# Hybrid attention trunk: V of two head groups in 512-column products, one value product per pair of heads, later steps, norm weights loaded elsewhere

## The chip, the core and the metric

The kernel runs on one core of a Trainium2 chip. Its engines are TensorE (PE in the profile, with PEld for its weight loads), VectorE (DVE), ScalarE (ACT), GpSimd (POOL) and SyncE (SP, which here only issues transfers). Each has its own instruction stream and works through it in order; they meet through semaphores. The metric is the device time of one execution in microseconds (us), lower is better. The kernel before takes 869.72 us, the median of three runs (869.27 to 870.09).

## The reference, cut to what matters

Two layers over 512 positions of width 1024, all float32. In each, one projection feeds three groups of heads:

```python
h = rms_norm(x, g_pre)
qa, ka, va, ga, qs, ks, vs, gs, qf, kf, vf, gf, ff = split(h @ w_in)      # 12 x 512 columns, and 8
# a) differential: 4 heads, rotary on part of q and k, two softmax maps each
w  = softmax(mask(q0 k0)) - lam * softmax(mask(q1 k1));  ya = rms_norm(w @ v) * (1 - lambda_init) * silu(ga)
# b) stick-breaking: 8 heads, strictly causal
a  = exp(log_sigmoid(z) + sum of log_sigmoid(-z) over later keys);        yb = (a @ v) * silu(gs)
# c) forgetting: 8 heads, causal softmax with a cumulative log gate as bias
p  = softmax(q k * scale + cum_q - cum_k);                                yc = (p @ v) * silu(gf)
x  = x + rms_norm(concat(ya, yb, yc) @ w_out, g_post)
```

## The kernel before, in words

A layer runs through stages named after the group whose columns are being projected: a, c, b, then the gates, then the output projection. `hT` holds the normalised input, transposed, as a high and a low part, and so does each weight; one product is three matmuls (`mm3`, L200 to L202). `proj_N` makes V 256 columns at a time for 128 positions, in eight chunks of the inner dimension; `proj_V` makes 512 columns at a time, and before the change only group b used it. `proj_T` makes q and k transposed, 128 columns by 512 positions. Every accumulation has one of three PSUM buffers `pj`.

Weights come in "halves" of 512 KB: a transfer on SP's queue into `raw` (3 buffers), a copy on ACT that rounds it to the high part (`split_to`, L184), and on POOL four subtractions for the low part (L190), into `hl` (4 buffers). A V unit for `proj_V` is four such halves, each with two chunks of the inner dimension.

While one group is projected, the attention steps of the group before run in between: 16 steps, four heads or pairs of heads by four blocks `i` of 128 queries. A step makes scores (L364), works on them on DVE and ACT, turns the weights with PE transposes into PSUM (L372), and an eviction writes them to SBUF (`pT`; group c: ACT for the first head, DVE at L377 for the second). Then `pair_av` multiplies them by v (L462, plain float32, the two heads on two halves of the array): before the change once for the blocks 0 and 1 and once for 2 and 3, with 256 columns. In stage a the rotary embedding keeps DVE busy (L328 to L332), ACT then writes the high part of q or k (L344) and DVE the low part (L349).

The order on every engine is written out by hand: `do` puts projection work in a row with a cost, `at` hangs side work at a time on that axis, and all is sorted by time. `use` says when a half is first needed, and its `lead` how much earlier its split is hung in. So a number in the code sets the order of instructions, not a time on the chip.

At the start `first_gain` loads the row of norm weights and spreads it over the partitions by matmul (L607); for the post norm `new_post` loads the weights that the evictions of the output projection need (L791).

Of the kernel before, what the change touches and what calls it, by code (L numbers as in the profile page):

```python
# [17 lines left out]
S = 512  # L18
# [42 lines left out]
def hybrid_kernel(ctx, tc, x, w_in, forget_bias, diff_lambda, diff_subln, w_out, pre_norm, post_norm, consts, out):  # L61
# [10 lines left out]
    t2_p = P("t2", T2_BUFS)  # L72
    pt0_p = P("pT0", 2)
    pt1_p = P("pT1", 2)
    cb_p = P("cb", 2)
# [32 lines left out]
    def load_rope():  # L108
        a, b = CONST_COLS["rope"]
        C["rope"] = pt1_p.tile([128, 2, S], F32, name="rope", tag="pT1")  # L110
        nc.sync.dma_start(out=C["rope"], in_=consts[:, a:b])
# [126 lines left out]

    def proj_V(k0, tt, hT, done):

        st = {}
        sl = slice(tt * 128, (tt + 1) * 128)

        def go(q):
            if q == 0:
                st["ps"] = pj_p.tile([128, S], F32, name="pj", tag="pj")
            h = hT()
            for kc in range(2 * q, 2 * q + 2):
                u = halves[k0 + q]["hl"][:, :, kc % 2]
                mm3(st["ps"], h[0][:, kc, sl], h[1][:, kc, sl], u[:, 0], u[:, 1], kc == 0, kc == KC - 1)  # L250

        for q in range(4):
            do(1296, lambda q=q: go(q))
        at(now[0], lambda: done(st["ps"]))

# [60 lines left out]

    def load_gain(g, src):
        for h, t in enumerate(g):
            nc.sync.dma_start(out=t, in_=src[h * S:(h + 1) * S].partition_broadcast(128))

# [79 lines left out]
    def step_a(t, c, h, i):  # L400
# [16 lines left out]
        def turn():  # L417
            st["t"] = t = pt0_p.tile([128, 4, 128], F32, name="wT", tag="pT0")
            transposed(st["p", 0], i, t[:, 0:i + 1], "act")
# [29 lines left out]
    def turned(c, pi, m, i):  # L449

        if i % 2 == 0:
            c["t", pi, i // 2, m] = (pt0_p if i == 0 else pt1_p).tile([128, i + 2, 256], F32, name="pT", tag=f"pT{i // 2}")
        return c["t", pi, i // 2, m][:, 0:i + 1, (i % 2) * 128:(i % 2 + 1) * 128]

    def pair_av(c, v, oT, pi, i, gated=False):
        ts = [c["t", pi, i // 2, m] for m in range(2)]
        o = ov_p.tile([128, 256], F32, name="ov", tag="ov")
        for j in range(i + 1):
            q0 = 128 if j == i else 0
            for m in range(2):  # L460
# [3 lines left out]
        d = oT[:, pi, (i - 1) * 128:(i + 1) * 128]  # L464
# [43 lines left out]
    def step_b(t, c, pi, i):  # L508
# [32 lines left out]
        for m in range(2):  # L541
# [5 lines left out]
            at(d + 5400, lambda m=m: turn(m))  # L547
        if i % 2:
            ta = max(t + 10900, c["gate"][pi])
            at(ta, lambda: pair_av(c, v(), oT(), pi, i, gated=True))  # L550
            if i == NT - 1:
                at(ta + 1200, lambda: c["cut"](pi))

# [36 lines left out]
    def first_norm(L):  # L590
# [7 lines left out]
        def first_gain():  # L598

            row = pt1_p.tile([1, 2, S], F32, name="grow", tag="pT1")  # L600
            nc.scalar.dma_start(out=row.rearrange("p h c -> p (h c)"), in_=pre_norm[0:1])
# [10 lines left out]
        t = -40000  # L612
        at(t, lambda: nc.vector.memset(mhalf, -0.5))
        at(t, lambda: load(0))
        at(t, first_gain)
        at(t, lambda: load_to(1))
        at(t, load_ident)
        at(t, lambda: L["st", 0].update(g=L["g"]))
# [13 lines left out]
    def plan_layer(l, L):  # L632
# [9 lines left out]
        for g in ("a", "c", "b"):  # L642
# [8 lines left out]
            if prev is not None:  # L651
                pst, pc, pg = prev
                at(t0, lambda pst=pst: pst.update(o=o_p.tile([128, 4, S], F32, name="o" + pg, tag="o")))
                steps(step_a if pg == "a" else step_c, pc, t0 + (3518 if pg == "a" else 3191), 50075 if pg == "a" else 46774)
            order = [(u, tt) for u in range(2) for tt in range(NT)]
            if g == "a":
                order = [(0, 0), (0, 1), (0, 2), (1, 0), (1, 1), (1, 2), (0, 3), (1, 3)]
            ks = []
            if g == "b":
                order = []  # L660
                kv = add_v_unit(l, base + 1024)
                for h in range(4):
                    use(kv + h, now[0] + 1296 * h)
                for tt in range(NT):
                    proj_V(kv, tt, hT, lambda ps, st=st, tt=tt: nc.scalar.activation(out=st["v"][:, tt], in_=ps, func=AF.Copy))
            for u in range(2 if g != "b" else 0):
                ks.append(add_in_unit(l, base + 1024 + u * UW, 6144 if g == "a" and u == 0 else None))
# [26 lines left out]
            for u in range(2):  # L694
                for part in ("q", "k"):
# [6 lines left out]
                    if g == "b" and u == 0 and part == "q":  # L702
                        for h in range(2):
                            halves[k0 + h]["lead"] = (3800, 5100)[h]
# [65 lines left out]
        for u, (g, j0) in enumerate(order):  # L770
            k = add_out_unit(l, row[g] + j0, 0, whl_p, "whl")
            use(k, now[0])
            for jj in range(2):
                for tt in range(NT) if (u, jj) == (5, 1) else (3, 0, 1, 2):
# [9 lines left out]
                    if u == 5 and jj == 1:  # L784
                        def ev(tt=tt):
                            if tt % 2 == 0:
                                L["yh"] = pt1_p.tile([128, 2, S], F32, name="y0", tag="pT1")
                            L["y0", tt] = t = L["yh"][:, tt % 2]
# [28 lines left out]
        for tt in range(NT):  # L817
# [98 lines left out]
```

## Time and profile before

| what | value |
|---|---|
| median of three runs | 869.72 us |
| profiled execution | 870.16 us, of which the span 868.1 us |
| TensorE busy, matmuls | 852.5 us (98%), 4700 instructions |
| VectorE busy | 496.4 us (57%) |
| ScalarE busy | 475.9 us (55%) |
| GpSimd busy | 447.7 us (52%) |
| mean granted TensorE clock | 0.998 |

The span goes from the first to the last instruction. A row of the timeline gives start, duration, engine, line, operation and tiles; "x8" after it says that eight like instructions are merged in the row, and brackets at its end give the engine's idle time before it and what ended it. Durations of neighbouring matmuls overlap, so what a matmul costs is read from the distance between two starts. A float32 matmul of `pair_av` shows as two instructions.

### The profile page before, as it was taken

To read this page: it belongs to the slowest core of one execution; us is meant where nothing else is said; L and a number is where in the kernel's file an instruction comes from. 1 tells how busy PE (TensorE), PEld (TensorE's weight loads), DVE (VectorE), ACT (ScalarE), POOL (GpSimd) and SP (SyncE) were. 2 spreads that over 40 slices of the span, in tenths; PEclk is the share of its full clock that TensorE was granted. 3 is DMA by queue.
4 is the path that set the end of the run, shared out by engine and by line. 5 is a ranking of instruction groups with operands and counts; after the bars stand their busy time and mean duration, and the time that the engine had idled before them with its cause. 6 is when DMAs were issued, how large, how long until landed. Compare 5 with 4: busy or idle time off the path is not lost.

```text
span 868.1 us, 13536 instructions
## 1 busy us (share of the span) xinstructions
PE 852.5 (98%) x4700; PEld 711.0 (82%) x4700; DVE 496.4 (57%) x1143; ACT 475.9 (55%) x1056; POOL 447.7 (52%) x678
## 2 busy tenths in 40 slices
PE   7999999999999999999999999999999999999997
PEld 5988998888878787788898889888888787877885
DVE  5378656544555777623653875664445477774322
ACT  4344667757775556633334356675677756664310
POOL 3366554645544548770364664556274544678301
PEclk9999999999999999999999999999999999999999
DMA  7354323432523321237253452325244422122522
GB/s 236 96 163 134 94 81 91 118 101 80 154 76 105 85 61 53 71 117 247 96 177 98 122 146 74 98 73 162 59 131 113 120 54 71 49 81 89 167 100 97
DMA packets 71157, 94.24 MB, mean 109 GB/s; under 512 B 6433, under 2 KB 52129, under 8 KB 71090
## 3 DMA queue, kind: packets, MB, share of 16 engines
q1 hardware_dynamic: 68784, 89.19, 35.2%
q10 hardware_dynamic: 2306, 4.20, 1.6%
q8 instruction: 37, 0.61, 0.3%
q14 instruction: 30, 0.25, 0.1%
HBM read 76.56 MB, written 4.23 MB: 93 GB/s over the span
## 4 chain that ended last, share of the span: by engine, by line
PE 81%; DVE 10%; ACT 3%; DMA 2%; issue 2%; POOL 1%; DVEq 0%; POOLq 0%; ACTq 0%
PE pj L200 18%; PE pj L202 18%; PE pj L201 18%; PE s L364 7%; PE pt L372 5%; PE ov L462 5%; PE acc L200 2%; PE acc L202 2%; PE acc L201 2%; PE ov L424 2%; DVE ra L332 2%; DVE sh L331 2%; DVE sh L328 1%; DVE qd L349 1%; DVE ra L330 1%
## 5 line engine op out<-in xcount | busy, mean ns | idle before, releaser
L190 POOL TENSOR_TENSOR hl<-raw,hl 128x256 fp32r<-128x256 f32 (+1 forms) x418 | 341.1, 848 | 217.4 <-ACT hl L184 193.2
L200 PE MATMUL pj<-hT,hl 128*128 128x512 f32 x576 | 236.4, 410 | 0.0
L202 PE MATMUL pj<-hT,hl 128*128 128x512 f32 x576 | 225.7, 392 | 0.0
L201 PE MATMUL pj<-hT,hl 128*128 128x512 f32 x576 | 225.2, 391 | 0.0
L184 ACT ACTIVATE hl<-raw 128x1024 fp32r<-128x1024 f32 (+1 forms) x120 | 126.3, 1058 | 35.2 <-DMA raw<-in_w_out_dram 18.7
L202 PEld LDWEIGHTS pj<-hT,hl 128*128 128x128 f32 x576 | 108.1, 188 | 24.2
L200 PEld LDWEIGHTS pj<-hT,hl 128*128 128x128 f32 x576 | 108.4, 188 | 20.0 <-issue 2.1
L201 PEld LDWEIGHTS pj<-hT,hl 128*128 128x128 f32 x576 | 108.7, 189 | 17.0
L200 PE MATMUL pj<-hl,hT 128*128 128x256 f32 (+2 forms) x320 | 101.0, 316 | 0.3 <-ACT hT L282 0.2
L202 PE MATMUL pj<-hl,hT 128*128 128x256 f32 (+2 forms) x320 | 98.4, 308 | 0.5 <-DVE hT L283 0.5
L201 PE MATMUL pj<-hl,hT 128*128 128x256 f32 (+2 forms) x320 | 98.2, 307 | 0.0
L398 ACT ACTIVATE p<-p,mn 128x128 f32<-128x128 f32 (+3 forms) x128 | 71.0, 555 | 33.0 <-DVE mn L389 31.1
L531 DVE TENSOR_TENSOR_SCAN kp<-kp,c_masks 128x128 f32<-128x128 f32 (+3 forms) x64 | 67.3, 1051 | 18.6 <-ACT kp L524 18.1
L364 PE MATMUL s<-kd,qd 128*128 128x128 f32 (+1 forms) x192 | 61.9, 327 | 2.8 <-DVE mn L389 2.8
L200 PEld LDWEIGHTS pj<-hl,hT 128*128 128x128 f32 x320 | 61.4, 192 | 3.4 <-ACT hT L282 1.0
L202 PEld LDWEIGHTS pj<-hl,hT 128*128 128x128 f32 x320 | 61.1, 191 | 3.8 <-DVE hT L283 1.2
L375 ACT ACTIVATE pT<-pt 128x128 f32<-128x128 f32 (+3 forms) x96 | 41.2, 443 | 41.8 <-PE pt L372 41.6
L201 PEld LDWEIGHTS pj<-hl,hT 128*128 128x128 f32 x320 | 61.4, 192 | 2.6 <-POOL hl L190 0.6
L364 PE MATMUL s<-kd,qs 128*128 128x128 f32 (+1 forms) x192 | 61.1, 322 | 0.0
L536 DVE TENSOR_TENSOR sg<-sg,kp 128x127 f32<-128x127 f32 (+3 forms) x64 | 46.1, 720 | 5.5
L481 POOL TENSOR_TENSOR cm<-cb,c_causal 128x128 f32<-128x128 f32 x64 | 28.2, 461 | 38.6 <-DMA cb<-cs 21.2
L193 DVE TENSOR_TENSOR hl<-raw,hl 128x1024 fp32r<-128x1024 f32 (+3 forms) x18 | 21.4, 1199 | 44.7 <-ACT hl L184 44.5
(143 smaller groups left out, 1456.9 us busy)
## 6 DMA issues: line engine op xcount, KB each, us to landing
raw<-in_w_in_dram SPq DMA_DIRECT2D x96, 512.0 KB, 3.7
qs<-qd SPq DMA_DIRECT2D x48, 256.0 KB, 4.3
raw<-in_w_out_dram SPq DMA_DIRECT2D x24, 512.0 KB, 3.5
cb<-cs ACTq DMA_DIRECT2D x16, 256.0 KB, 3.2
xl<-in_x_dram SPq DMA_DIRECT2D x4, 512.0 KB, 5.4
xt<-in_x_dram SPq DMA_DIRECT2D x8, 256.0 KB, 6.3
xs<-xt SPq DMA_DIRECT2D x8, 256.0 KB, 2.0
xt<-xs SPq DMA_DIRECT2D x8, 256.0 KB, 2.8
```

The source lines that it names most:

```text
L184: nc.scalar.activation(out=hl[:, 0], in_=raw, func=AF.Copy)
L190: nc.gpsimd.tensor_tensor(out=hl[:, 1, k, c:e], in0=raw[:, k, c:e], in1=hl[:, 0, k, c:e].bitcast(F32), op=ALU.subtract)
L200: nc.tensor.matmul(out=ps, lhsT=lh, rhs=rh, start=first, stop=False)
L201: nc.tensor.matmul(out=ps, lhsT=lh, rhs=rl, start=False, stop=False)
L202: nc.tensor.matmul(out=ps, lhsT=ll, rhs=rh, start=False, stop=last)
L364: nc.tensor.matmul(out=s[:, 0:n], lhsT=pr[q][:, m, i * 128:n], rhs=pr["k"][:, m, 0:n], start=(j == 0), stop=(j == 1))
L372: nc.tensor.transpose(out=pt[:, j * 128:(j + 1) * 128], in_=p[:, j * 128:(j + 1) * 128], identity=C["ident"])
L375: nc.scalar.activation(out=t, in_=src, func=AF.Copy)
L398: nc.scalar.activation(out=p[:, 0:n], in_=p[:, 0:n], func=AF.Exp, bias=st["mn", m], scale=-1.0, accum_out=su)
L462: nc.tensor.matmul(out=o[H[m], q0:256], lhsT=v[:, j, col:col + 64], rhs=ts[m][:, j, q0:256], start=(j == 0), stop=(j == i))
L531: nc.vector.tensor_tensor_scan(out=rv, data0=rv, data1=C["first"][:, S - n:S][:, ::-1], initial=0.0, op0=ALU.mult, op1=ALU.max)
L536: nc.vector.tensor_tensor(out=sg[:, 0:n - 1], in0=sg[:, 0:n - 1], in1=kp[:, 1:n], op=ALU.mult)
```

## The change

Group c's V is made by `proj_V` too, so 256-column products of that group become half as many of 512 columns; group a keeps `proj_N`. `proj_V` takes two blocks of positions at a time and goes over the first half of the inner dimension for both before it goes on to the second half, and the leads of the third and fourth half of the unit change (at the same places on the axis as before for group b, whose use is later now). `pair_av` runs once per pair of heads with up to 512 columns, on weights that lie in one tile per head. The differential steps start 2982 units later in stage c and are 2775 units shorter in all; the forgetting steps turn their weights 1339 units later, and their value product comes 7600 units after the start of the last step. Three pools of SBUF become one. The first norm row goes on SP's queue, ahead of x, the identity ahead of the first weights; the post-norm weights go on ACT's queue and 3000 units earlier; the next layer's norm transposes come 949 units later.

```diff
-    def proj_V(k0, tt, hT, done):
+    def proj_V(k0, tts, hT, done):
...
+        for q in (0, 2):
+            for tt in tts:
+                for j in range(2):
+                    do(1296, lambda tt=tt, q=q + j: go(tt, q))
+                if q == 2:
+                    at(now[0], lambda tt=tt: done(ps[tt], tt))
...
     def turned(c, pi, m, i):
-        if i % 2 == 0:
-            c["t", pi, i // 2, m] = (pt0_p if i == 0 else pt1_p).tile([128, i + 2, 256], F32, name="pT", tag=f"pT{i // 2}")
-        return c["t", pi, i // 2, m][:, 0:i + 1, (i % 2) * 128:(i % 2 + 1) * 128]
-
-    def pair_av(c, v, oT, pi, i, gated=False):
-        ts = [c["t", pi, i // 2, m] for m in range(2)]
-        o = ov_p.tile([128, 256], F32, name="ov", tag="ov")
-        for j in range(i + 1):
-            q0 = 128 if j == i else 0
+        if i == 0:
+            c["t", pi, m] = pt_w.tile([128, 13 * 128], F32, name="pT", tag="pT")
+        d = c["t", pi, m][:, i * 128:(i + 1) * 128]
+        return bass.AP(tensor=d.tensor, offset=d.offset, ap=[d.ap[0], [384, i + 1], [1, 128]])
+
+    def pair_av(c, v, oT, pi, gated=False):
+        ts = [c["t", pi, m] for m in range(2)]
+        o = ov_p.tile([128, S], F32, name="ov", tag="ov")
+        for j in range(NT):
             for m in range(2):
                 col = (2 * pi + m) * 64
-                nc.tensor.matmul(out=o[H[m], q0:256], lhsT=v[:, j, col:col + 64], rhs=ts[m][:, j, q0:256],
-                                 start=(j == 0), stop=(j == i))
+                nc.tensor.matmul(out=o[H[m], j * 128:S], lhsT=v[:, j, col:col + 64],
+                                 rhs=ts[m][:, j * 512:j * 384 + 512], start=(j == 0), stop=(j == NT - 1))
...
-            at(d + 4261, lambda m=m: turn(m))
-        if i % 2:
-            at(t + 9959, lambda: pair_av(c, v(), oT(), pi, i))
+            at(d + 5600, lambda m=m: turn(m))
+        if i == NT - 1:
+            at(t + 7600, lambda: pair_av(c, v(), oT(), pi))
...
-            ta = max(t + 10900, c["gate"][pi])
+            ta = max(t + 8500, c["gate"][pi])
...
-        at(t, lambda: load(0))
         at(t, first_gain)
+        at(t, lambda: load(0))
+        at(t, load_ident)
         at(t, lambda: load_to(1))
-        at(t, load_ident)
...
-                steps(step_a if pg == "a" else step_c, pc, t0 + (3518 if pg == "a" else 3191), 50075 if pg == "a" else 46774)
+                steps(step_a if pg == "a" else step_c, pc, t0 + (6500 if pg == "a" else 3191), 47300 if pg == "a" else 46774)
...
-            if g == "b":
+            if g != "a":
                 order = []
                 kv = add_v_unit(l, base + 1024)
+                by = 2
                 for h in range(4):
-                    use(kv + h, now[0] + 1296 * h)
+                    if by == 2:
+                        halves[kv + h]["lead"] = (9500, 8000, 7700, 6400)[h]
+                    use(kv + h, now[0] + 1296 * (h + (2 if by == 2 and h > 1 else 0)))
...
-            load_gain(gains["post"], post_norm[l])
-        at(now[0] - 9000, new_post)
+            load_gain(gains["post"], post_norm[l], nc.scalar)
+        at(now[0] - 12000, new_post)
...
-                for d, fn in zip((2500, 4500, 4600, 7551, 8326), pre_norm_stages(st, tt, N["hT"])):
+                for d, fn in zip((2500, 4500, 4600, 8500, 9275), pre_norm_stages(st, tt, N["hT"])):
```

What moves on ACT at the passage from stage a to stage c of the first layer: `kd` is the high part of a k projection (the third and the fourth of the last two units), `hl` with L184 or L183 a half of V's weights, `v` an eviction of V. Before:

```order
L344 ACTIVATE kd_878<-ra_861 64x512 x2
L184 ACTIVATE hl_916<-raw_763 128x1024
L344 ACTIVATE kd_936<-ra_897 64x512 x2
L681 ACTIVATE v_901<-pj_903 128x256
L184 ACTIVATE hl_961<-raw_823 128x1024
```

And now:

```order
L346 ACTIVATE kd_875<-ra_858 64x512 x2
L183 ACTIVATE hl_884<-raw_760 128x1024
L183 ACTIVATE hl_915<-raw_820 128x1024
L346 ACTIVATE kd_929<-ra_902 64x512 x2
L400 ACT_TABLE_LOAD
```

The third half of V stands where it stood, behind the last but one k; the fourth now stands next to it, ahead of the last k.

PE at the same place, one row for each half of the weights as it is first used by a block of positions (hl_817, 845, 916 and 961 are the four halves before, hl_814, 842, 884 and 915 now; `pj` with a new number is a new accumulation, `s` are the first scores of the differential steps). Before:

```order
L200 MATMUL pj_903<-hl_817,hT0_145 128x256
...
L200 MATMUL pj_903<-hl_845,hT0_145 128x256
...
L364 MATMUL s_955<-kd_696,qd_594 128x128
...
L364 MATMUL s_981<-kd_696,qd_594 128x128
...
L364 MATMUL s_1005<-kd_696,qd_594 128x256
```

And now:

```order
L199 MATMUL pj_908<-hl_814,hT0_142 128x512
...
L199 MATMUL pj_908<-hl_842,hT0_142 128x512
...
L199 MATMUL pj_932<-hl_814,hT0_142 128x512
...
L199 MATMUL pj_908<-hl_884,hT0_142 128x512
...
L199 MATMUL pj_908<-hl_915,hT0_142 128x512
...
L366 MATMUL s_959<-kd_693,qd_591 128x128
...
L199 MATMUL pj_932<-hl_884,hT0_142 128x512
```

Before, the third half was first used after all four blocks of positions had used the first two, 96 products of 256 columns on; now it is used after two blocks, 24 products of 512 columns on, and the fourth half 6 products later. The first scores now come after both.

PE around a value product of group c in stage b (`pt` the transposes of the second head's last block, `ov` the value product, `s` scores of the next pair). Before, the second of two products of a pair:

```order
L462 MATMUL ov_2587<-pT_2395,v_901 64x256
L462 MATMUL ov_2587<-pT_2405,v_901 64x256
...
L462 MATMUL ov_2587<-pT_2395,v_901 64x128
L462 MATMUL ov_2587<-pT_2405,v_901 64x128
```

And now, the only one:

```order
L374 MATMUL pt_2384<-c_masks_128,p_2281 128x128 x4
L366 MATMUL s_2395<-kd_1682,qd_1449 128x256
L366 MATMUL s_2395<-kd_1682,qs_1475 128x256
L199 MATMUL pj_2292<-hl_2060,hT0_142 128x512
...
L464 MATMUL ov_2422<-pT_2220,v_906 64x512
L464 MATMUL ov_2422<-pT_2234,v_906 64x512
L464 MATMUL ov_2422<-pT_2220,v_906 64x384
L464 MATMUL ov_2422<-pT_2234,v_906 64x384
```

Between the last transposes and the value product there now stand two score matmuls of 256 columns and six products of 512.

## Rows read from the trace of the kernel before

**Rows 1.** The page: busy time by engine, and the granted clock in 40 slices.

```profile
PE 852.5 (98%) x4700; PEld 711.0 (82%) x4700; DVE 496.4 (57%) x1143; ACT 475.9 (55%) x1056; POOL 447.7 (52%) x678
PEclk9999999999999999999999999999999999999999
```

**Rows 2.** Waits of PE, one line: for whom, us in total, times, longest.

```profile
PE s L364 <- DVE mn L389: 2.8, 2, 1.7
```

**Rows 3.** Timeline of PE: V in 256 columns, products 1 and 24; 512 columns, 11 in a row.

```profile
36.70 0.28 PE L200 MATMUL pj<-hl,hT 128*128 128x256 f32 x1
...
39.45 0.28 PE L202 MATMUL pj<-hl,hT 128*128 128x256 f32 x1
...
195.66 0.39 PE L201 MATMUL pj<-hl,hT 128*128 128x512 f32 x1
...
197.96 0.39 PE L202 MATMUL pj<-hl,hT 128*128 128x512 f32 x1
```

**Rows 4.** Timeline of PE: two value products, what stands before and behind them.

```profile
208.77 1.74 PE L462 MATMUL ov<-pT,v 128*64 128x256 f32 x16
210.44 0.66 PE L372 MATMUL pt<-c_masks,p 128*128 128x128 f32 x4
...
287.26 0.40 PE L202 MATMUL pj<-hT,hl 128*128 128x512 f32 x1
287.58 0.87 PE L462 MATMUL ov<-pT,v 128*64 128x256 f32 x8
288.38 0.50 PE L200 MATMUL pj<-hT,hl 128*128 128x512 f32 x1
288.72 0.40 PE L201 MATMUL pj<-hT,hl 128*128 128x512 f32 x1
```

**Rows 5.** Timeline, all engines: from stage a to c in layer one, then two.

```profile
83.59 0.28 PE L200 MATMUL pj<-hl,hT 128*128 128x256 f32 x1
84.42 1.28 ACT L344 ACTIVATE kd<-ra 64x512 fp32r<-64x512 f32 x2 [3.24 <-DVE ra L332]
85.72 1.06 ACT L184 ACTIVATE hl<-raw 128x1024 fp32r<-128x1024 f32 x1
86.86 3.72 POOL L190 TENSOR_TENSOR hl<-raw,hl 128x256 fp32r<-128x256 f32 x4 [1.88 <-ACT hl L184]
92.47 0.38 PE L364 MATMUL s<-kd,qd 128*128 128x256 f32 x1 [1.09 <-DVE mn L389]
92.87 2.84 POOL L190 TENSOR_TENSOR hl<-raw,hl 128x256 fp32r<-128x256 f32 x4 [2.30 <-ACT hl L184]
...
508.39 0.28 PE L200 MATMUL pj<-hl,hT 128*128 128x256 f32 x1
512.32 3.73 POOL L190 TENSOR_TENSOR hl<-raw,hl 128x256 fp32r<-128x256 f32 x4 [1.89 <-ACT hl L184]
517.93 0.38 PE L364 MATMUL s<-kd,qd 128*128 128x256 f32 x1 [1.75 <-DVE mn L389]
```

**Rows 6.** Timeline: PE behind post-norm weights, then ahead of layer two.

```profile
403.93 0.50 PE L200 MATMUL pj<-hl,yv 128*128 128x512 f32 x1 [0.25 <-DVE y L791]
...
439.40 0.63 PE L279 MATMUL pt<-c_masks,xn 128*128 128x128 f32 x4 [0.66 <-DVE xn L273]
```

**Rows 7.** Timeline of SP's queue: issues of the first x and of the identity.

```profile
0.72 0.39 SPq L594 DMA_DIRECT2D xl<-in_x_dram  x1
...
2.97 0.51 SPq L106 DMA_DIRECT2D c_masks<-in_consts_dram  x1
```

**Rows 8.** Timeline: last transposes of two forgetting pairs, and their eviction on DVE.

```profile
201.30 0.62 PE L372 MATMUL pt<-c_masks,p 128*128 128x128 f32 x4
201.96 0.69 DVE L377 COPY pT<-pt 128x512 f32<-128x512 f32 x1
...
221.12 0.62 PE L372 MATMUL pt<-c_masks,p 128*128 128x128 f32 x4
222.97 0.69 DVE L377 COPY pT<-pt 128x512 f32<-128x512 f32 x1
```

More of the change, by code (lines that the diff above doesn't have):

```diff
@@ L72, in hybrid_kernel @@
     t2_p = P("t2", T2_BUFS)
-    pt0_p = P("pT0", 2)
-    pt1_p = P("pT1", 2)
+    pt_w = P("pT", 2)
     cb_p = P("cb", 2)
@@ L109, in load_rope @@
         a, b = CONST_COLS["rope"]
-        C["rope"] = pt1_p.tile([128, 2, S], F32, name="rope", tag="pT1")
+        C["rope"] = pt_w.tile([128, 2, S], F32, name="rope", tag="pT")
         nc.sync.dma_start(out=C["rope"], in_=consts[:, a:b])
@@ L237, in proj_N, with go @@
             at(now[0] + t, fn)
-    def proj_V(k0, tt, hT, done):
-        st = {}
-        sl = slice(tt * 128, (tt + 1) * 128)
-        def go(q):
+    def proj_V(k0, tts, hT, done):
+        ps = {}
+        def go(tt, q):
             if q == 0:
-                st["ps"] = pj_p.tile([128, S], F32, name="pj", tag="pj")
+                ps[tt] = pj_p.tile([128, S], F32, name="pj", tag="pj")
             h = hT()
+            sl = slice(tt * 128, (tt + 1) * 128)
             for kc in range(2 * q, 2 * q + 2):
                 u = halves[k0 + q]["hl"][:, :, kc % 2]
[L250 to L254, printed above, removed]
+                mm3(ps[tt], h[0][:, kc, sl], h[1][:, kc, sl], u[:, 0], u[:, 1], kc == 0, kc == KC - 1)
+        for q in (0, 2):
[4 more added lines that the diff above has]
+                    at(now[0], lambda tt=tt: done(ps[tt], tt))
     def pre_norm_stages(st, tt, hT):
@@ L315, in new_gain, with load_gain @@
         return [t[:, 0], t[:, 1]]
-    def load_gain(g, src):
+    def load_gain(g, src, eng=nc.sync):
         for h, t in enumerate(g):
-            nc.sync.dma_start(out=t, in_=src[h * S:(h + 1) * S].partition_broadcast(128))
+            eng.dma_start(out=t, in_=src[h * S:(h + 1) * S].partition_broadcast(128))
     H = (slice(0, 64), slice(64, 128))
@@ L417, in turn @@
         def turn():
-            st["t"] = t = pt0_p.tile([128, 4, 128], F32, name="wT", tag="pT0")
+            st["t"] = t = pt_w.tile([128, 4, 128], F32, name="wT", tag="pT")
             transposed(st["p", 0], i, t[:, 0:i + 1], "act")
@@ L547, in step_b @@
             at(d + 5400, lambda m=m: turn(m))
-        if i % 2:
-            ta = max(t + 10900, c["gate"][pi])
-            at(ta, lambda: pair_av(c, v(), oT(), pi, i, gated=True))
-            if i == NT - 1:
-                at(ta + 1200, lambda: c["cut"](pi))
+        if i == NT - 1:
+            ta = max(t + 8500, c["gate"][pi])
+            at(ta, lambda: pair_av(c, v(), oT(), pi, gated=True))
+            at(ta + 2000, lambda: c["cut"](pi))
     def decay(ff, lc, l):
@@ L598, in first_gain @@
         def first_gain():
-            row = pt1_p.tile([1, 2, S], F32, name="grow", tag="pT1")
-            nc.scalar.dma_start(out=row.rearrange("p h c -> p (h c)"), in_=pre_norm[0:1])
+            row = pt_w.tile([1, 2, S], F32, name="grow", tag="pT")
+            nc.sync.dma_start(out=row.rearrange("p h c -> p (h c)"), in_=pre_norm[0:1])
             one = t1_p.tile([1, 128], F32, name="one", tag="on")
@@ L613, in first_norm @@
         at(t, lambda: nc.vector.memset(mhalf, -0.5))
+        at(t, first_gain)
         at(t, lambda: load(0))
-        at(t, first_gain)
+        at(t, load_ident)
         at(t, lambda: load_to(1))
-        at(t, load_ident)
         at(t, lambda: L["st", 0].update(g=L["g"]))
@@ L658, in plan_layer @@
             ks = []
-            if g == "b":
+            if g != "a":
                 order = []
                 kv = add_v_unit(l, base + 1024)
+                by = 2
                 for h in range(4):
-                    use(kv + h, now[0] + 1296 * h)
-                for tt in range(NT):
-                    proj_V(kv, tt, hT, lambda ps, st=st, tt=tt: nc.scalar.activation(out=st["v"][:, tt], in_=ps, func=AF.Copy))
-            for u in range(2 if g != "b" else 0):
+                    if by == 2:
+                        halves[kv + h]["lead"] = (9500, 8000, 7700, 6400)[h]
+                    use(kv + h, now[0] + 1296 * (h + (2 if by == 2 and h > 1 else 0)))
+                for t_ in range(0, NT, by):
+                    proj_V(kv, range(t_, t_ + by), hT,
+                           lambda ps, tt, st=st: nc.scalar.activation(out=st["v"][:, tt], in_=ps, func=AF.Copy))
+            for u in range(2 if g == "a" else 0):
                 ks.append(add_in_unit(l, base + 1024 + u * UW, 6144 if g == "a" and u == 0 else None))
@@ L701, in plan_layer @@
                             halves[k0 + h].update(lead=2500, lo="both")
-                    if g == "b" and u == 0 and part == "q":
+                    if g != "a" and u == 0 and part == "q":
                         for h in range(2):
@@ L786, in ev @@
                             if tt % 2 == 0:
-                                L["yh"] = pt1_p.tile([128, 2, S], F32, name="y0", tag="pT1")
+                                L["yh"] = pt_w.tile([128, 2, S], F32, name="y0", tag="pT")
                             L["y0", tt] = t = L["yh"][:, tt % 2]
```

2 lines of the change are left out of this document (1 added, 1 removed).

## The prediction

> **What bounds the kernel now.** I read the page first: TensorE's matmuls are busy for 852.5 of the span's 868.1 us, at full granted clock (2.4 GHz) in every slice, while VectorE, ScalarE and GpSimd stand at 52 to 57% [rows 1]. So the kernel is bound by the row of instructions on PE: whatever shortens that row, or a wait in it, comes off the time one for one, and what happens elsewhere counts only where PE comes to wait for it. Next I read PE's waits: the largest that the change touches is that of the scores L364 for DVE, 2.8 us in two waits [rows 2]. Then the timeline of PE, for what one instruction costs there (distances between starts, since durations overlap). Last the timeline of all engines at the passage from stage a to c, because there the change moves weights and work at once.
>
> **The change part by part.**
>
> *V of group c.* Per layer 192 products of 256 columns become 96 of 512. From product 1 to product 24 in 256 columns it is 39.45 - 36.70 = 2.75 us in 23 steps, 0.1196 us each; in 512 columns 2.30 us in 10 steps, 0.230 each [rows 3]. Two layers: 384 x 0.1196 = 45.9 against 192 x 0.230 = 44.2, so -1.7 us, all on PE's row.
>
> *One value product per pair.* There were 32 groups (two for each of 4 pairs, 2 head groups, 2 layers), now 16. The columns are the same in sum, 384 + 896 = 1280 per head. A group of 384 took 288.38 - 287.58 = 0.80 us, one of 896 took 210.44 - 208.77 = 1.67 [rows 4]; that is 1.70 ns per column and 0.15 us that each group pays whatever its size. Around it PE pays for going in, 287.58 - 287.26 = 0.32 where 0.23 is usual, and for coming out into a product, 288.72 - 288.38 = 0.34 where 0.23 is usual [rows 3, 4]: 0.09 and 0.11. A group saved is worth 0.24 (where transposes follow, whose own extra I put at nothing) to 0.35 us, so 3.8 to 5.6 for 16; I take -5.2, nearer the upper end, because by the order all 16 that remain are followed by products, and of the 32 old ones 18 by products or scores and 14 by transposes. No row shows a float32 product of 512 columns. If width has a price of its own, the gain could be nothing; that is the other end.
>
> *Differential steps later.* The two waits of L364 on DVE are 1.09 and 1.75 us of idle time [rows 5]; a score there starts 0.16 us later still than the idle time says, because a product of 256 lasts 0.28 but is followed after 0.12 [rows 3]. Together -3.1 us. DVE is through with the rotary work in both layers before the scores in their new place come, so this wait goes.
>
> *What is late next there.* This is the step that decides. PE begins V of group c at 83.59 us. The third half of the weights is split by ACT only at 85.72, right behind the k that waited 3.24 us for DVE, and POOL subtracts from 86.86 to 90.58 [rows 5]. Before, PE wanted that half after 96 products; now it wants it after 24 products of 512, and the fourth after 30. ACT's order keeps the third half where it was and puts the fourth next to it, ahead of the last k. POOL then goes straight on with the fourth half: another 2.84 us (the row at 92.87) or 3.72 (the row at 86.86), so it ends at 93.4 to 94.3. PE, were it not held, would need its last piece after 33 products, at 83.59 + 33 x 0.230 = 91.2. So PE is held for 2.2 to 3.1 us. In the second layer the start is 508.39 and POOL ends with the third half at 512.32 + 3.73 = 516.05 [rows 5]; the same sum gives 518.9 to 519.8 against 516.0, 2.9 to 3.8 us. Together 5.1 to 6.9; I take +5.7. If ACT or POOL came to these halves earlier than the order says, it would be nothing.
>
> *Post-norm weights and norm transposes.* PE idled 0.25 us for L791, which waited for the weights' transfer, and 0.66 us in the transposes L279 [rows 6]; a product of 512 lasts 0.39 and is followed after 0.23 [rows 3], so each costs 0.16 more: 0.4 and 0.8. The weights now come 3000 units earlier (13 products) and the transposes 949 units later (4 products, 0.9 us), so both go: -1.2 us. The two issues on ACT's queue stand in the output projection, where PE waits for no ACT work in the rows; if they did not hide there, they would cost twice the 0.5 us of such an issue [rows 7].
>
> *Start.* One more issue stands on SP's queue ahead of x. Issues of this kind took 0.39 and 0.51 us [rows 7], and x is what everything at the start waits for: +0.45. The identity ahead of the first weights delays them by 0.5 more, and if that counts too it is 0.9; if the earlier row of weights helps, nothing.
>
> *Forgetting steps.* Turning later costs nothing by itself. But the value product follows its last transposes closely now: 0.46 for these (0.62 less the 0.16 of overlap), two scores of 0.12, six products of 0.23 and 0.09 for going in, 2.2 us from the start of the transposes. The eviction on DVE ended 1.35 us after that start in one pair (201.30 to 202.65) and 2.54 in another (221.12 to 223.66) [rows 8]. So the wait is 0 or 0.34 us; for eight such groups 0 to 2.7, and I take +0.4, since the shorter lag is the usual one. Stick-breaking has by the order some five products more there in three pairs of four and is hidden. The merged pools and the two blocks at a time in V of group b change no order that PE waits on: its halves are split where they were and used later.
>
> Sum: -1.7 - 5.2 - 3.1 + 5.7 - 1.2 + 0.45 + 0.4 = -4.65. The profiled execution took 870.16 us (span 868.1 and 2.06 around it), 0.44 above the median of 869.72. Off the median the forecast is 865.1 us, or 865.5 for an execution like the profiled one.
>
> **The rivals.**
>
> *The halves come in time.* If ACT reaches the third and fourth half before the k that waits for DVE, or DVE is further along, the +5.7 falls away: -10.35, 859.4 us. For it speaks that POOL idled 1.88 us before the third half; against it that ACT works in order and stood still for DVE until 84.42 [rows 5].
>
> *Both halves at the slow pace.* A group of four subtractions took 3.72 us beside DVE's rotary work and 2.84 without it [rows 5]. While POOL does the fourth half, DVE still has the low part of the last k to do, so 3.72 may hold for it too: 6.9 instead of 5.7, 866.3 us. The Trainium skill, SBUF — State Buffer, section Who interferes with whom, says that a DVE instruction with two inputs in SBUF holds up a GpSimd instruction that reads SBUF, and the other way round, for a whole instruction; the trace agrees with it in the two durations, and by that rule it would be this case.
>
> *Slower: the value product waits for POOL.* In stage b the diagonal bias of the next scores is added on POOL, behind weight splits of 2.84 us, and DVE, in order, then makes the eviction late; the copy at 222.97 came 1.0 us later after its transposes than that at 201.96 [rows 8] for a reason of this kind. Should each of the eight forgetting groups find a whole split in front, its eviction ends 1.35 + 2.84 = 4.2 us after the transposes and PE waits 2.0: 16 in place of 0.4, 880.7 us. From 0.85 us a group on, the kernel is slower than before. Against it: the larger lag shown is 2.5, not 4.2.
>
> *The wide value product saves nothing.* Without the -5.2 it is +0.55, 870.3 us.
>
> **How the numbers follow.** The forecast gets 0.53, its own range being 862.5 to 867.5; the halves in time 0.20; the slow pace 0.15; waiting for POOL 0.07; no gain from width 0.05. The range goes from 859.4, the first rival, to 867.9, which leaves out the last two and little else. A measurement of this kernel can tell 0.2%, some 1.7 us. Faster by more than that: the first three, less a little of their upper tail, 0.87; within it 0.06; slower 0.07.
>
> **What would show it.** L200 to L202 in 256 columns 384 fewer, and 16 groups of the value product, each near 2.3 us. No wait of L364 for DVE; in its place waits of L200 and L201 for POOL's subtraction in the first blocks of V of group c, 2 to 4 us in each layer. The first transposes 0.4 to 0.5 us later. No wait at L791's release. If PE shows no wait for POOL there, the forecast is wrong and the first rival right; if a group of the value product stays above 2.5 us or starts behind a wait for the eviction, the last two are.

## The result, and the profile after

The changed kernel takes 881.32 us, the median of four runs (880.05 to 884.92), against 869.70 us (869.27 to 870.09): 1.0138 times the time before, 95% interval 1.0125 to 1.0151. It is slower; 865.1 us was forecast. The profiled execution took 880.05 us, its span is 878.1, 10.0 more than before.

First the span in stages, by the start of PE's first product in each: layer one, V of group c, the q and k products of c, V of group b, and the stretch from there to the output projection. Columns: span, then busy time and instructions of PE, weight loads, DVE, ACT and POOL, granted clock, DMA share, GB/s. Before:

```profile
83.59:115.14 31.55, 30.37 (x250) 29.79 (x248) 17.97 (x57) 20.35 (x53) 16.24 (x24) 1.00 0.31 89
115.14:177.41 62.27, 62.27 (x337) 53.17 (x336) 40.03 (x125) 42.46 (x115) 34.30 (x59) 1.00 0.39 105
177.41:207.29 29.88, 29.88 (x157) 24.72 (x156) 12.65 (x61) 19.02 (x48) 13.39 (x25) 1.00 0.21 66
207.29:370.46 163.17, 163.14 (x903) 129.52 (x903) 104.11 (x218) 104.84 (x230) 96.69 (x149) 1.00 0.32 91
```

After:

```profile
84.37:115.03 30.66, 28.44 (x141) 23.11 (x140) 17.03 (x49) 18.07 (x45) 13.60 (x19) 1.00 0.22 59
115.03:184.59 69.56, 65.21 (x348) 53.89 (x347) 40.86 (x132) 44.47 (x120) 37.47 (x66) 1.00 0.40 109
184.59:215.82 31.23, 31.23 (x165) 25.18 (x164) 13.06 (x62) 18.82 (x47) 15.89 (x28) 1.00 0.26 79
215.82:376.10 160.28, 159.82 (x834) 125.61 (x833) 100.03 (x210) 104.69 (x230) 91.27 (x143) 1.00 0.32 90
```

The loss is in the first two rows: stage c grew from 93.82 to 100.22 us, and PE's idle time in its q and k products from 0 to 4.35. The other two rows together shrank, from 193.05 to 191.51. In layer two stage c grew from 94.50 to 101.79.

PE's waits of the changed kernel (whom for, us in total, times, longest) against [rows 2]:

```profile
PE pj L200 <- POOL hl L189: 4.7, 7, 0.9
PE pt L374 <- DVE p L416: 4.4, 6, 1.0
PE pt L442 <- DVE oc L443: 2.9, 4, 0.7
...
PE pt L374 <- ACT wT L377: 1.2, 2, 0.6
...
PE s L366 <- DVE mn L391: 0.9, 2, 0.5
```

The first line is the wait for the weight halves that was forecast (one of the seven, 0.3 us, stands at the start of the kernel). The two waits of the scores for DVE, 2.8 us, are gone; the 0.9 in the last line (L366 is the old L364) are two new ones of 0.46, in the forgetting steps, shown below. The second, third and fourth line were not forecast: transposes of the differential steps, L374 for the weights and L442 for the output, that wait for DVE and ACT. But DVE is 55% busy. What it waits for there, before and after:

```profile
DVE on L427 <- PE pt L440: 17.7, 12, 4.5
```

```profile
DVE on L429 <- PE pt L442: 38.0, 16, 4.5
```

`on` is the output row of a differential step, and has three buffers. L429 writes it at 7856 units of a step, L442 reads it last at 17029. Where three steps follow each other within 9173 units, DVE's write of step n+3 stands, by the order, behind a transpose of step n that PE has further down its row. By the step lengths in the code three steps took 8450 to 10328 units before, under 9173 at 7 of 13 places in a layer; now they take 7982 to 9756, under it at 10. One such place in the timeline, ACT, DVE and PE in turn (start, duration, instruction, idle time before it); the row of ACT is the normalisation of `on`, which had waited for GpSimd, and two of the experiments are about that:

```profile
118.58 0.40 ACT L438 ACTIVATE on<-on,rsub 128x128 f32<-128x128 f32 x1 [2.98 <-POOL rsub L126]
```

```profile
121.44 0.35 DVE L429 TENSOR_SCALAR on<-ov,r 128x128 f32<-128x128 f32 x1 [3.38 <-PE pt L442]
121.71 0.15 DVE L411 RECIPROCAL r<-su 128x1 f32<-128x1 f32 x1
...
122.69 0.91 DVE L416 SCALAR_TENSOR_TENSOR p<-p,rho 128x256 f32<-128x256 f32 x1
...
124.48 0.34 DVE L443 TENSOR_SCALAR oc<-pt,sub 128x128 f32<-128x128 f32 x1
```

```profile
121.13 0.27 PE L442 MATMUL pt<-c_masks,on 128*128 128x128 f32 x1
...
123.75 0.41 PE L374 MATMUL pt<-c_masks,p 128*128 128x128 f32 x2 [0.95 <-DVE p L416]
124.87 0.33 PE L442 MATMUL pt<-c_masks,on 128*128 128x128 f32 x1 [0.72 <-DVE oc L443]
```

DVE stands still for 3.38 us until PE reaches L442 at 121.13, and then has the reciprocals, L416 and two score reductions to do in a row. PE, six products further, comes to the transposes that need them and waits twice. So PE waits for an engine that had waited for PE.

The wait that was forecast in V of group c, on PE and on POOL:

```profile
90.49 0.39 PE L199 MATMUL pj<-hl,hT 128*128 128x512 f32 x1
91.38 0.50 PE L200 MATMUL pj<-hl,hT 128*128 128x512 f32 x1 [0.50 <-POOL hl L189]
...
93.21 0.50 PE L200 MATMUL pj<-hl,hT 128*128 128x512 f32 x1 [0.87 <-POOL hl L189]
...
95.03 0.50 PE L200 MATMUL pj<-hl,hT 128*128 128x512 f32 x1 [0.85 <-POOL hl L189]
```

```profile
87.61 7.37 POOL L189 TENSOR_TENSOR hl<-raw,hl 128x256 fp32r<-128x256 f32 x8 [1.89 <-ACT hl L183]
```

By starts, against 0.23 a product, PE loses 0.66, 1.04 and 1.02 us: 2.7 a layer. The product behind each wait is followed after 0.34 in place of 0.23, which makes it 3.0. And one value product of a pair of heads, which answers to [rows 4]:

```profile
211.30 2.37 PE L464 MATMUL ov<-pT,v 128*64 128x512 f32 x16
213.60 0.50 PE L199 MATMUL pj<-hl,hT 128*128 128x512 f32 x1
```

One wait was not forecast there either, in the forgetting steps, on POOL, DVE and PE:

```profile
226.30 2.81 POOL L189 TENSOR_TENSOR hl<-raw,hl 128x256 fp32r<-128x256 f32 x4 [1.87 <-ACT hl L183]
229.07 2.12 POOL L483 TENSOR_TENSOR cm<-cb,c_causal 128x128 f32<-128x128 f32 x5
```

```profile
229.56 0.29 DVE L391 CUSTOM_DVE_ANT_0 p<-s,cm 128x128 f32<-128x128 f32 x1 [0.81 <-POOL cm L483]
```

```profile
229.92 0.39 PE L366 MATMUL s<-kd,qd 128*128 128x256 f32 x1 [0.46 <-DVE mn L391]
```

The diagonal bias `cm` stands on POOL behind a weight split, DVE waits for it, and the next scores on PE wait for DVE: once in each layer.

### The profile page after: what moved, and what is told of

It is laid out like the page before. It is cut to its first block, busy times and chain, and to the rows that moved or that the text cites. A ratio compares the mean times of both kernels' runs of the same rounds, so it can differ in the third digit from the quotient of the medians.

```text
span 878.1 us, 12845 instructions
## 1 busy us (share of the span) xinstructions
PE 852.6 (97%) x4380; PEld 694.8 (79%) x4380; DVE 487.2 (55%) x1127; ACT 474.3 (54%) x1048; POOL 443.4 (50%) x678
## 4 chain that ended last, share of the span: by engine, by line
PE 78%; POOL 10%; issue 6%; DVE 3%; ACT 2%; DMA 1%; SPq 0%; DVEq 0%; POOLq 0%; ACTq 0%
PE pj L199 18%; PE pj L201 17%; PE pj L200 17%; POOL hl L189 9%; PE s L366 6%; PE pt L374 5%; PE ov L464 4%; PE acc L199 2%; PE acc L200 2%; PE acc L201 2%; PE ov L426 2%; ACT hl L183 1%; DVE p L391 1%; DVE p L416 1%; DMA raw<-in_w_in_dram 1%
## 5 line engine op out<-in xcount | busy, mean ns | idle before, releaser
L199 PE MATMUL pj<-hT,hl 128*128 128x512 f32 x576 | 236.6, 411 | 0.0
L183 ACT ACTIVATE hl<-raw 128x1024 fp32r<-128x1024 f32 (+1 forms) x120 | 125.8, 1056 | 39.5 <-DMA raw<-in_w_out_dram 21.9
L199 PEld LDWEIGHTS pj<-hT,hl 128*128 128x128 f32 x576 | 108.6, 188 | 21.0 <-issue 2.4
L200 PE MATMUL pj<-hl,hT 128*128 128x512 f32 (+2 forms) x256 | 88.7, 346 | 4.7 <-POOL hl L189 4.7
L199 PE MATMUL pj<-hl,hT 128*128 128x512 f32 (+2 forms) x256 | 91.0, 356 | 1.0 <-ACT hT L284 1.0
L400 ACT ACTIVATE p<-p,mn 128x128 f32<-128x128 f32 (+3 forms) x128 | 71.0, 555 | 36.1 <-DVE mn L391 35.3
L201 PE MATMUL pj<-hl,hT 128*128 128x512 f32 (+2 forms) x256 | 88.2, 344 | 0.4 <-DVE hT L285 0.4
L366 PE MATMUL s<-kd,qd 128*128 128x128 f32 (+1 forms) x192 | 63.6, 335 | 0.9 <-DVE mn L391 0.9
L366 PE MATMUL s<-kd,qs 128*128 128x128 f32 (+1 forms) x192 | 61.4, 324 | 0.0
L200 PEld LDWEIGHTS pj<-hl,hT 128*128 128x128 f32 x256 | 49.7, 194 | 11.2 <-POOL hl L189 7.6
L199 PEld LDWEIGHTS pj<-hl,hT 128*128 128x128 f32 x256 | 49.8, 195 | 6.8 <-ACT hT L284 1.9
L201 PEld LDWEIGHTS pj<-hl,hT 128*128 128x128 f32 x256 | 49.6, 194 | 6.0 <-DVE hT L285 0.9
L493 ACT ACTIVATE p<-p,rc 128x128 f32<-128x128 f32 (+3 forms) x64 | 35.2, 556 | 26.9 <-DVE rc L491 26.8
L124 POOL TENSOR_SCALAR msub<-ssa 128x1 f32<-128x1 f32 x32 | 9.4, 295 | 76.5 <-ACT oj L434 75.7
```

Source lines behind the costliest of these rows:

```text
L183: nc.scalar.activation(out=hl[:, 0], in_=raw, func=AF.Copy)
L199: nc.tensor.matmul(out=ps, lhsT=lh, rhs=rh, start=first, stop=False)
L200: nc.tensor.matmul(out=ps, lhsT=lh, rhs=rl, start=False, stop=False)
L201: nc.tensor.matmul(out=ps, lhsT=ll, rhs=rh, start=False, stop=last)
L366: nc.tensor.matmul(out=s[:, 0:n], lhsT=pr[q][:, m, i * 128:n], rhs=pr["k"][:, m, 0:n], start=(j == 0), stop=(j == 1))
L400: nc.scalar.activation(out=p[:, 0:n], in_=p[:, 0:n], func=AF.Exp, bias=st["mn", m], scale=-1.0, accum_out=su)
```

## The experiments

Times are medians; the kernel before ran beside each group of runs and took 869.8 to 869.9 us. The numbers in brackets are the 95% interval of the ratio to it.

**The steps where they were.** In the changed kernel:

```diff
-t0 + (6500 if pg == "a" else 3191), 47300 if pg == "a" else 46774
+t0 + (3518 if pg == "a" else 3191), 50075 if pg == "a" else 46774
```

> The changed kernel with the differential steps of group a where they stood before (first at 3518, spread over 50075 units); all else of the change stays. Theory (the squeezed steps cost it): the 5.8 us per layer in which PE waits for DVE among the q and k products of group c go, the two waits of the scores L364 for DVE come back (2.8 us idle), so 881.3 - 11.6 + 3.1 = about 873 us, and 867 to 870 if the other 1.5 us per layer by which that stretch grew go too. Rival (it is V of c in 512 columns, or the late weight halves, that pushes DVE's work into these steps): the time stays within 878 to 884.

867.78 us (0.9967 to 0.9987): 13.5 us of the 11.6 lost are undone by this line. It is less than the 873 worked out from the waits. The q and k products of c are back at 62.46 us, so their whole growth is gone, and there is a second reason:

```profile
PE s L366 <- DVE mn L391: 4.9, 4, 2.0
```

The wait of the scores for DVE is back at its old place and larger, 1.97 us in each layer (the other two of the four are the new ones in the forgetting steps); the wait of V of c for POOL's halves is not in the list. The scores stand in the row just where the halves were late, so one hole of 2.1 us covers both. In this kernel the +5.7 and the 3.1 of the sum are not two terms, but one.

**The later start with the old spread.** Only 47300 is put back to 50075.

> The changed kernel with the later first step (6500) but the old spread (50075 units). Theory (the spread decides: three steps must not follow within 9173 units, or VectorE's write to the buffer `on` waits for the transposes that read it): most of the 11.6 us go and the waits of L364 stay away, 867 to 871 us. Rival (the shift by 2982 units decides, since it puts the steps against the splits of the weights in another phase): 878 to 884 us.

873.59 us (1.0028 to 1.0058), between the two, so neither was right. The spread matters, but the start does too.

**The transposes back earlier.** In the changed kernel:

```diff
-(9775, norm), (17029, back)
+(9775, norm), (15500, back)
```

> The changed kernel, its steps where the change puts them (6500, 47300), but the transposes back (L442) at 15500 units of each step in place of 17029, so that they stand in PE's row ahead of the output row of the step three later, which writes the same buffer `on`. Theory (the buffer `on` is what DVE waits for): the wait of DVE L429 for PE L442 (38.0 us in 16 waits) goes or falls below 15, and the time falls to 867 to 872 us. Rival (DVE is late because the squeezed steps hold too much work, whatever the buffer): the wait goes and the time stays within 877 to 884.

868.15 us (0.9972 to 0.9995). The steps stand as squeezed as in the changed kernel, and 13.2 us are gone. DVE's longest wait at L429 is now the product just ahead of it:

```profile
DVE on L429 <- PE ov L426: 20.4, 20, 2.5
```

PE's waits in the transposes fell from 8.5 us to 0.2, and the q and k products of c from 69.56 to 64.05. What VectorE has to do in these steps is the same. With 15500 the buffer is held for 7644 units, less than any three steps take. So the wait for `on` is the cause, and not the amount of work. The edit also puts the transposes at another place in PE's row; that this place alone gains nothing is shown by the same edit in the kernel before, below. A fourth buffer for `on` would be the more direct test; no run has it.

**The steps alone.** The kernel before, with 6500 and 47300.

> The kernel before with the new place of the differential steps alone (6500, 47300). Theory (the squeezed steps cost by themselves): slower, 869.7 - 3.1 + 11.6 to 14 = 878 to 881 us, with waits of the transposes L372 and L440 for DVE among the q and k products of group c. Rival (they cost only together with V of c in 512 columns): the waits of L364 go and nothing comes, 866 to 868 us, as the prediction had this step by itself.

877.87 us (1.0074 to 1.0104), just under the theory's range: 8.0 slower by these two numbers, with the waits of the theory (L279 belongs to the norm at the start of a layer):

```profile
PE pt L440 <- DVE oc L441: 2.9, 4, 0.7
PE pt L279 <- DVE xn L273: 2.7, 3, 1.1
PE pt L372 <- DVE p L414: 2.5, 4, 0.7
```

**The steps alone, with the transposes back at 15500.**

> The kernel before with the differential steps where the change puts them (6500, 47300) and the transposes back at 15500; nothing else. This is the prediction's term of 3.1 us by itself, with the wait for the buffer `on` taken away. Theory: 869.8 - 3.1 = 866.7 us, V of group c 28.6 us long and its q and k products about 64. Rival (squeezed steps cost whatever the buffer): 871 to 877 us, near the 877.9 of the steps alone.

866.54 us (0.9937 to 0.9970): 3.4 faster than before, where the prediction had 3.1 for the step. One number in the code turns -3.4 into +8.0: the wait for `on` costs 11.3 us in the kernel before and 13.2 in the changed one.

**The transposes back at 15500 in the kernel before.**

> The kernel before with the transposes back at 15500 in place of 17029 and nothing else. Theory (the wait of DVE for them, 17.7 us in 12 waits, costs the kernel before nothing, since PE does not come to wait): the wait goes and the time stays at 869 to 870.5 us. Rival (it already holds DVE back, and with it the scores' releases): 864 to 868 us.

871.15 us (1.0002 to 1.0021), 1.3 slower and a little above the theory's range. The wait for L440 is gone and nothing is gained, so DVE's 17.7 us of waiting cost the kernel before nothing. That it could catch up because the steps stood further apart is the likely reading, not a measured one. In the profiled execution V of c of layer two is 33.59 us in place of 32.22, at a granted clock of 0.949 behind a wait of the scores of 1.97 us (1.75 before); more on that at the end.

**The old spread, later, with the transposes early.** As the second run, with back at 15500.

> The changed kernel with the first step at 6500, the old spread of 50075 (873.6 us so far) and the transposes back at 15500. Theory (with the old spread it is the same wait for `on`, 11.7 us in 8 waits, on which PE comes to wait in the new phase): 867 to 869 us, like the squeezed steps with the transposes early (868.2). Rival (the phase against the other work costs, not the buffer): 872 to 874 us.

874.86 us (1.0036 to 1.0065), so here the theory failed: there is no wait of L429 for L442 left, and the time did not move. POOL, ACT, DVE and PE at the place where PE loses most:

```profile
120.07 2.99 POOL L189 TENSOR_TENSOR hl<-raw,hl 128x256 fp32r<-128x256 f32 x4 [1.46 <-ACT hl L183]
123.15 0.19 POOL L124 TENSOR_SCALAR msub<-ssa 128x1 f32<-128x1 f32 x1
123.43 0.55 POOL L126 TENSOR_TENSOR rsub<-msub,mhalf 128x1 f32<-128x1 f32 x1
```

```profile
124.01 0.40 ACT L438 ACTIVATE on<-on,rsub 128x128 f32<-128x128 f32 x1 [2.58 <-POOL rsub L126]
124.32 0.60 ACT L400 ACTIVATE p<-p,mn 128x384 f32<-128x384 f32 x1
```

```profile
127.94 1.41 DVE L351 SCALAR_TENSOR_TENSOR qd<-pj,qd 64x512 fp32r<-64x512 f32 x2 [1.23 <-ACT qd L346]
129.38 0.35 DVE L429 TENSOR_SCALAR on<-ov,r 128x128 f32<-128x128 f32 x1
```

```profile
129.79 0.71 PE L426 MATMUL ov<-v,wT 128*128 128x128 f32 x4 [1.04 <-DVE on L429]
```

The two small instructions for the norm stand on POOL behind a weight split of 2.99 us. ACT's L438 waits for them, the exponentials L400 wait behind L438, and DVE and PE come late in turn.

**The normalisation later.** The same kernel, with L438 behind those exponentials.

```diff
-(9775, norm), (15500, back)
+(12500, norm), (15500, back)
```

> The changed kernel with the first step at 6500, the old spread of 50075, the transposes back at 15500 (874.9 us so far) and the normalisation L438 on ScalarE at 12500 units of each step in place of 9775, behind the exponentials that it held up. Theory (ScalarE's wait for GpSimd's small instructions behind a weight split makes DVE late): the two waits of PE per layer go, 868 to 870 us. Rival (VectorE's rotary work of 1.4 us stands in front of the step's own at the wrong moments, whatever ScalarE does): 873 to 876 us.

868.07 us (0.9969 to 0.9989), 6.8 less, in the theory's range. PE's wait of L426 for L429 is gone, and the q and k products of c are 64.20 us in place of 66.79. So there are two ways to the same end, and which one decides depends on where the steps stand.

**The normalisation later in the changed kernel,** back at 17029.

> The changed kernel with the normalisation L438 at 12500 units of each step in place of 9775, nothing else. Theory (the wait of VectorE for the transposes back, by the buffer `on`, makes the loss by itself): no gain, 879 to 885 us, with L429 waiting for L442 some 38 us as before. Rival (the late normalisation ahead of it starts the loss): 868 to 874 us.

877.56 us (1.0070 to 1.0116). The wait for `on` stays, and with it most of the loss; the q and k products of c are 68.5 us in place of 69.6, so the norm's share there is about 1 us a layer. The median is 3.8 lower, just under the range that the theory gave, so the wait for `on` does not make quite all of the loss by itself.

```profile
DVE on L429 <- PE pt L442: 38.4, 16, 4.6
```

**V of group c.** All with back at 15500 (868.15 us). First the third half split earlier on ACT:

```diff
-halves[kv + h]["lead"] = (9500, 8000, 7700, 6400)[h]
+halves[kv + h]["lead"] = (9500, 8000, 9000, 6400)[h] if g == "c" else (9500, 8000, 7700, 6400)[h]
```

> The changed kernel with the transposes back at 15500, as in the run of that name (868.2 us), and in group c the lead of V's third weight half at 9000 in place of 7700, so that ScalarE splits it one k earlier. Theory (what is left is PE's wait for POOL's subtractions in V of group c, 2.72 us by starts in each layer): it falls to 0 to 1 us a layer, 862.5 to 865 us. Rival (POOL's pace or the k it then delays decides): the wait stays or comes back at another place, 867 to 870 us.

863.39 us (0.9913 to 0.9946). One wait of 1.0 us is left in each layer. Then V of c in 256 columns, as before:

> The changed kernel with the transposes back at 15500 (868.2 us) and V of group c in 256 columns, as before the change. Theory (V of c in 512 columns gains 0.85 us a layer in products and loses 2.7 by the late halves): 868.2 + 1.7 - 5.4 = about 864.5 us, no wait of PE for POOL in V of group c. Rival (the halves' wait only stands where another would be: without it PE waits for DVE there): 867 to 870 us.

862.37 us (0.9899 to 0.9928), with no wait there, 2.1 below the theory. So the wider products of V of c, as the change has them, cost 5.8 us by the medians and 4.5 between the two profiled executions; in the slower executions of 868.15 the granted clock is lower, down to 0.992. Even with the third half on time the wider products are no gain. Last, all three later halves one k or q earlier (leads 11500, 10300, 10300, 10300, so the first half moves too), and the first loads in the old order:

> The changed kernel with the transposes back at 15500, the first loads in the old order, and all three later weight halves of V of group c split on ScalarE one k or q earlier (leads 10300), V of c in 512 columns. Theory (GpSimd then starts the halves up to 1.9 us sooner, and the last 1.0 us of wait a layer goes): 863.4 - 2.0 - 0.6 = 860.8 us, under the kernel with V of c in 256 columns (861.8), as 0.85 us a layer in products should make it. Rival (DVE or the buffers of the halves hold GpSimd, or the k that now comes later does): 862 to 865 us.

862.53 us (0.9884 to 0.9925). No wait for POOL is left; V of c is 28.34 and 28.99 us in the two layers, against 28.61 and 28.62 in 256 columns, because the wait of the scores for DVE came back, `PE s L366` for L391 at 2.5 us in 4 waits where it had been 0.9. What is saved on the products is lost there.

**The value products alone.** The kernel before, with the grouped value products, the later turns and the shared pool (one pool for `pT` in place of two).

> The kernel before with the value products of a pair of heads in one group, the turns of the forgetting steps and the shared pool that go with it, and V of group b two blocks at a time; the differential steps, V of c, the norm weights and the start as before. By starts of the 16 groups against the 32 the gain is 2.8 us in the groups and 1.4 on the way in, 4.2 in all, and 3.3 to 4.0 by the length of the stretch of groups b and c: 865.5 to 866.5 us. Rival (the shared pool or the later turns make PE wait): 868 to 871 us. The prediction's term was 5.2: 864.5.

868.30 us, but from 866.36 to 872.96 (0.9974 to 1.0008), so the median decides nothing. The profiled execution of 870.56 us had a wait of 3.1 us of the output projection for the post-norm weights (`PE pj L199` for L796), which the change moves to an earlier place; the two parts of that projection took 4.5 us more than before. The stretch from V of b to the output projection shrank from 193.05 to 191.39 us in layer one and from 193.02 to 191.50 in layer two, 3.2 in all. The gain of the value products is read from the traces, below.

**The best version.** Steps as in the change, transposes back at 15500, V of c and the first loads as before.

> The changed kernel with the transposes back at 15500, V of group c in 256 columns as before (862.4 us so far), and the order of the first loads as before the change: x ahead of the row of norm weights, that row on ScalarE's queue, the identity after the first weights. Theory (the start costs 0.6 us: PE's first product of V of group a stands at 8.5 to 8.9 us with the old order and at 9.0 to 9.7 with the new): 861.8 us. Rival (nothing hangs on it): 862.4.

861.90 us (0.9884 to 0.9917), the fastest that ran: 8.0 under before, 19.4 under the change.

## Why the prediction was wrong

The step that failed is "Differential steps later". It took away the wait of the scores for DVE, -3.1 us, and saw rightly that all of it goes. But it asked only what DVE has done by then, and put what the moved steps do to one another at nothing. Alone that step is +8.0 us (877.87). The sum named stage c as the place that decides, and looked for the new wait at the weights alone. The trace of before held the warning: DVE's 12 waits at L427 for PE's L440, 17.7 us. It cost nothing while the steps stood further apart.

With that wait taken out (transposes back at 15500) stage c by itself is what the sum had. It predicted -1.7 - 3.1 + 5.7 = +0.9 for both layers; the two stages are 94.72 and 94.69 us against 93.83 and 94.50, +1.1. The kernel is still 3.0 over the forecast there (868.15): the value products with the forgetting steps were put at -4.8 and brought -3.3 in its trace, and its profiled execution, at a mean granted clock of 0.998, is 1.3 below its median, which slower executions with a lower clock raise.

- V of c, weights late: right in mechanism and size where the steps stand later, 2.7 a layer, or 3.0 with the slower starts behind the waits, against 2.85. POOL worked through the two halves in 7.37 us, 0.92 a subtraction, the pace of the row of 3.72 for four and not that of 2.84 [rows 5]. This pace would have given 3.1 and 3.8 by the prediction's sum; in layer two the halves were no later than in layer one. The Trainium skill, SBUF — State Buffer, section Who interferes with whom, says that a DVE instruction with two inputs in SBUF contends with a GpSimd instruction that reads SBUF; this pace of 0.92 us beside DVE's rotary work agrees with it.
- One value product per pair: 5.2 was too much. By starts, the 32 groups took 39.7 us and the 16 take 36.9; 16 ways in of 0.09 fall away besides [rows 3, 4]. That is 4.2. The way out was counted 16 times at 0.11, but all 16 groups that remain pay it, and of the 32 old ones only 18 did, so it falls away twice; the order that the prediction named as a reason for the upper end spoke for the lower. The stretch from V of b to the output projection shrank by only 1.5 us in each layer, 3.0 in all. Most of the rest is in the scores of that stretch, which by starts cost 1.1 us more in the two layers; the new wait stands there. Each group is 2.30 us, as forecast, and none of the 16 starts behind a wait.
- Forgetting steps: no value product waits, but the scores do, 0.46 us of idle time once in each layer, behind POOL's bias and a weight split of 2.81 us. The wait stands in every profiled run with the later turns and the grouped value products, the value products alone among them, and in none without; which part brings it was not tested. It is the mechanism of the prediction's slower case, at another instruction and at a fraction of its price. That this case had the time nearly right (880.7) is luck. It also read a lag of 1.0 us in [rows 8] that is 1.2 (1.85 against 0.66).
- Post-norm weights and norm transposes: both waits went. The two parts of the output projection in layer one fell from 33.47 and 35.86 us to 33.02 and 34.52, and 0.34 of that comes back in V of group a of layer two (24.59 to 24.93), where the later transposes now stand: 1.45 in all, where 1.2 was put.
- Start: PE's first product of V is at 9.54 us, 0.68 later, where 0.45 was put (0 to 0.9). The place was wrong: the first transposes of x stand at 7.06 us against 7.05, not 0.4 to 0.5 later. Late is the first half of the weights, which ACT splits at 7.92 in place of 6.29. Over all profiled runs the product stands at 8.5 to 9.0 us with the old order of the loads and at 9.0 to 9.8 with the new.

One cost of the forecast wait was not in the sum. In layer two of the changed kernel, behind the three waits in V of c, the granted clock fell (same columns as the first fence):

```profile
523.00:524.50 1.50, 1.27 (x6) 1.13 (x7) 0.08 (x1) 0.00 (x0) 0.17 (x1) 0.74 0.15 18
524.50:526.00 1.50, 1.50 (x6) 1.21 (x6) 0.52 (x4) 1.25 (x5) 0.00 (x0) 0.50 0.92 268
526.00:527.50 1.50, 1.50 (x7) 1.27 (x6) 0.00 (x0) 0.11 (x2) 0.00 (x0) 0.62 0.19 64
527.50:530.00 2.50, 2.50 (x14) 2.08 (x14) 2.21 (x12) 1.69 (x5) 0.00 (x0) 1.00 0.00 0
```

0.50 is the lower level, 1.2 GHz. Products there follow each other after 0.43 us in place of 0.23, and V of c took 32.24 us against 30.66 in layer one, 1.6 more.

What stays open is the share of each wait in the +8.0, since PE's waits in stage c overlap with work that is only moved, and what makes the clock fall in one layer and not in the other. A fourth buffer for `on` was not tried.

## What to carry to other kernels

Before steps of a software pipeline are moved closer together, take each rotating buffer and compare its lifetime, from the first write to the last read in the order of the slowest row, with the number of buffers times the new distance of the steps. A wait that costs nothing in the profile can be such a buffer already at its limit, as it was here with an engine at 57% that waited for the bottleneck; look there first. And when a wait goes, ask which other wait it covered: 2.1 us of waiting for DVE hid 2.7 us of waiting for weights.

## What the runs showed of the hardware

The same three waits of 0.5 to 0.9 us in V of c were followed by the lower clock in layer two of the changed kernel and not in layer one, at full clock before both. The later start with the old spread shows the fall in both layers; in the profiled execution of the changed kernel with the transposes early the same waits had none. The kernel before with the transposes early shows it behind a single wait of 1.97 us in V of c, the value products alone behind one of 3.1 us in the output projection. The single waits of 0.5 to 1.05 us in the q and k products of c were followed by it in no trace: the four executions of the steps alone, which have only those in stage c, lie 0.9 us apart (877.19 to 878.12). The four of the changed kernel, which has both kinds, lie 4.9 us apart, and those of the best version, without either, 0.3 (861.75 to 862.02). So in this kernel waits of PE in V of c cost their length and, at times, some 1.6 us more; what decides it stays open.
